# Gate/up in a hybrid encoder layer: five of seven Strassen products with a 512-column operand, six banks per unit, and 63 pieces' sums made in earlier stages

## The chip, the cores and the metric

The kernel runs on one core of one Trainium2 chip. The metric is the device time of one execution, in microseconds (us); lower is better. The time before is the median of three runs.

## The reference, cut to what matters

One layer over 512 tokens of width 2048, in float32: norm, one input projection, two mixers beside each other (dilated window attention with 16 heads of 64, and bidirectional gated linear attention with 4 heads), output projection, norm, and a SwiGLU block of hidden width 5632.

```python
h = rmsnorm(x, attn_norm_w)
aq, ak, av, gq, gk, gv, gr, glr = split(h @ w_in)
attn    = mixture_of_dilations(aq, ak, av, rel_bias_table)      # 16 heads
gla_out = rmsnorm_per_head(gla_fwd + gla_bwd) * gla_norm_w * silu(gr)   # 4 heads
x = x + concat(attn, gla_out) @ w_out
h = rmsnorm(x, ffn_norm_w)
x = x + (silu(h @ w_gate) * (h @ w_up)) @ w_down       # 2048 -> 5632 -> 2048
return rmsnorm(x, final_norm_w)
```

## The kernel before, in words

**Precision.** Every large product is made of three matmuls in a rounded 32-bit format (F32R in the code): an operand is split into a rounded part (hi) and the remainder (lo), and hi x hi, hi x lo and lo x hi are added in the same bank. ACT makes the hi part with a copy, DVE the lo part with a subtraction.

**Stages.** The program is one order of instructions, written out by hand. Jobs 0 to 15 (`run_job`) are the input projection (q/k, v, the operands of linear attention, its output gate) and the output projection. A job has 16 "halves": 128 rows of the weights times 512 columns, made from a 512 KB piece that `Stream` loads on SP's queue, at most three pieces ahead, and splits three halves ahead (L198 on ACT, L199 on DVE). Its products are L295 to L297 or L304 to L306, with 512 columns. Between two halves, `run_side` lets a queue of generators (`side`) make steps of attention or linear attention at a rate per job, and one step from `urgent`.

Job 6 starts at 344.3 us of the span, job 7 at 406.6, job 8 at 464.8, job 12 at 683.3, job 15 at 817.5. The steps in jobs 6 and 7 are the attention of heads 12 to 15, those of jobs 8 to 11 linear attention. Then comes gate/up (862.8 to 1752.6 us of the span), then the down projection and the last norm.

**Attention.** A step (`att_step`, h is the head and b one of its four blocks of queries) has the score matmuls (L573, L574), the score operation on DVE (L586), the transposes of the two steps before (L532) with copies by ACT (L598) and remainders by DVE (L599), the product with V (L540, L541), the exponential by ACT, the mix of an output (L550, L552) and the normalisation (L525, L526). Behind job 5, q and k parts of the last heads are split and copied into place by 24 DMAs on SP's queue (L483 to L495).

**Linear attention.** Per head, the reciprocal root of a mean square is made by a chain of small operations (L323 to L329), which scales an output tile on ACT (L885); TensorE then transposes that (L891).

**Gate/up.** `Feed` goes through 44 units, a 256-column strip of w_gate and one of w_up in turn, and each unit through 4 pieces of 512 x 256 weights. The product is a Strassen-Winograd one: 7 products of quarter blocks in place of 8. Of the weights, each piece needs sums of its blocks (`sums`, L1157 to L1159, three operations on DVE for four sums), and then the split of three blocks and four sums (L1170 on ACT, L1175 on DVE). Of x, `pair_operands` makes the sums and splits during the output projection. A piece has 2 x 7 products of three matmuls with 256 columns (L1216 to L1218):

```python
mm(o, wh, xh, ...)    # L1216
mm(o, wh, xl, ...)    # L1217
mm(o, wl, xh, ...)    # L1218
```

The seven products of a unit lie in four of the eight banks of PSUM, two halves of a bank side by side in three of them. At a unit's end `evac` (L1227, L1232, L1235) empties them in two steps from `urgent`, and a third (`finish`, L1253 to L1259) multiplies with the norm's factor, takes Silu (gate), or multiplies the two and stores the tile (`gd`). `run` sets the order: piece i's split, the sums of pieces i+1 and i+2, the split of i+1, products of i, then one step from `urgent`.

**Buffers.** `s4` has 16 buffers of 1024 columns (in the profile "b"), `s2` 70 of 512 columns ("a"), `ps` the 8 banks. A request takes a free buffer, and the instruction that fills it waits until the last user is done. Each engine and each queue works in its program order.

Of the kernel before, what the change touches and what calls it, by code (L numbers as in the profile page):

```python
# [117 lines left out]
def layer(nc, tc, x, attn_norm_w, w_in, rel_table, gw_f, gb_f, gw_b, gb_b, gla_norm_w, w_out,  # L118
# [7 lines left out]
    with tc.manual_schedule(), \  # L126
# [27 lines left out]
        state = {"credit": 0.0, "set": None}  # L154
# [96 lines left out]
        class Job:  # L251
# [3 lines left out]
            banks = None  # L255

# [11 lines left out]
        def run_job(j):  # L268
# [6 lines left out]
            for i in range(j.n):  # L275
# [754 lines left out]
        def pair_operands(q, fs_):  # L1030

            a, z = slice(0, 256), slice(256, 512)
            f1, f2 = fs_
            t13, t24 = s2.get(), s2.get()
            sub = lambda o, x_, y_: dve.tensor_tensor(o, x_, y_, op=OP.subtract)
            sub(t13.t[:, a], f1.t[:, a], f1.t[:, z])
            sub(t13.t[:, z], f2.t[:, z], f1.t[:, z])
            dve.tensor_tensor(t24.t[:, a], f2.t[:, z], t13.t[:, a], op=OP.add)
            sub(t24.t[:, z], t24.t[:, a], f2.t[:, a])
            yield  # L1040
            todo = []
            slots = []
            for src, n in ((f1.t[:, a], 256), (f2.t, 512), (t13.t, 512), (t24.t, 512)):
                sl, hi, lo, hf = half_split(src, n)
                slots += sl
                todo.append((src, hi, lo, hf))
            for i in range(4):
                src, hi, lo, hf = todo[i]
                act.copy(hi, src)
                sub(lo, src, hf)  # L1050
                put((f1, f2, t13, t24)[i])
                if i % 2:
                    yield
            (_, b1h, b1l, _), (_, f2h, f2l, _), (_, t13h, t13l, _), (_, t24h, t24l, _) = todo
            xs[q] = dict(slots=slots, B11=(b1h, b1l), B21=(f2h[:, a], f2l[:, a]), B22=(f2h[:, z], f2l[:, z]),
                         T1=(t13h[:, a], t13l[:, a]), T3=(t13h[:, z], t13l[:, z]),
                         T2=(t24h[:, a], t24l[:, a]), T4=(t24h[:, z], t24l[:, z]))
# [63 lines left out]
        class Blocks:  # L1121
# [10 lines left out]
            def load(self):  # L1132
                while self.n_load < self.n and len(self.raw) < self.most and s4.free:
                    w, k, n_kt, col, n = self.source(*self.seq[self.n_load])
                    r = s4.get(F32, self.shape(4))
                    sp.dma_start(out=r.t.rearrange("p a b c -> p (a b c)").rearrange("p (k c) -> p k c", k=n_kt),
                                 in_=w[k * P:(k + n_kt) * P, col:col + n].rearrange("(k p) c -> p k c", p=P))
                    self.raw[self.n_load] = r
                    self.n_load += 1

# [40 lines left out]
        class Feed(Blocks):  # L1181
# [3 lines left out]

            def __init__(self):
# [4 lines left out]
                self.begin(seq, 2, P)  # L1191

# [3 lines left out]

            def products(self, i, banks):
                st_ = self.sets.pop(i)
                piece = self.seq[i][1]
                first, last = piece == 0, piece == self.per - 1  # L1200
                a, z = slice(0, 256), slice(256, 512)
                A, B, C, E = (b.t for b in banks)
                for p in range(2):
                    q = 2 * piece + p
                    (rh, rl), (sh, sl) = st_
                    R = lambda n: (rh.t[:, p, n], rl.t[:, p, n])
                    Z = lambda n: (sh.t[:, p, n], sl.t[:, p, n])
                    x_ = xs[q]
                    prods = [(A[:, a], R(0), x_["B11"], True), (A[:, z], R(2), x_["B21"], False),
                             (B[:, a], Z(2), x_["T2"], True), (C[:, a], Z(1), x_["T1"], True),  # L1210
                             (C[:, z], Z(0), x_["T3"], False), (E[:, a], Z(3), x_["B22"], True),
                             (E[:, z], R(1), x_["T4"], False)]
                    for o, (wh, wl), (xh, xl), head in prods:
                        head = head and first and p == 0
                        end = last and p == 1
                        mm(o, wh, xh, start=head, stop=False, skip_group_check=True)  # L1216
                        mm(o, wh, xl, start=False, stop=False, skip_group_check=True)  # L1217
                        mm(o, wl, xh, start=False, stop=end, skip_group_check=True)  # L1218
                for hi, lo in st_:
                    put(hi, lo)  # L1220

            def evac(self, u, banks):
# [12 lines left out]
                dve.tensor_tensor(t1.t[:, z], t1.t[:, a], B[:, a], op=OP.subtract)  # L1235
                yield
# [7 lines left out]
                put(banks[1])  # L1244
                self.finish(u, c_, c)
                yield

            def finish(self, u, c_, c):
                w, j = self.units[u]
                if w is w_gate:  # L1250
                    tables(SILU)
                    for f in range(2):
                        dve.tensor_tensor(c_.t[:, f], c_.t[:, f], rb[2 + f].t, op=OP.mult)  # L1253
                    act.activation(c_.t, c_.t, AF.Silu)
                    self.gate = c_
                else:
                    dve.tensor_tensor(c_.t, c_.t, self.gate.t, op=OP.mult)
                    put(self.gate)
                    pool.dma_start(out=gd[j], in_=c)  # L1259
                    put(c_)  # L1260

            def run(self):
                banks = {}
                for i, (u, q) in enumerate(self.seq):
                    if u not in banks:
                        banks[u] = [ps.get() for _ in range(4)]
# [6 lines left out]
                    if i < 2:  # L1273
                        self.sums(self.n_sums, halves=True)
                    self.products(i, banks[u])
                    if u == len(self.units) - 1:
                        for p in (2 * q, 2 * q + 1):
                            put(*xs.pop(p)["slots"])
                        down_start(q)
                    for _ in range(3 if i < 2 else 2 if i < 8 else 1):  # L1280
                        run_urgent()
                    if q == self.per - 1:
                        urgent.append(self.evac(u, banks.pop(u)))
# [422 lines left out]
        run_last = finish()  # L1706
        for n, j in enumerate(jobs):
# [6 lines left out]
            if n == n_out:  # L1714
                ff.run()
# [29 lines left out]
```

## Time and profile before

| what | value |
|---|---|
| median of 3 runs | 2216.93 us (2216.35 to 2217.04) |
| the profiled execution | 2216.53 us |
| its span | 2214.8 us |
| mean granted TensorE clock | 0.999 |
| TensorE busy | 2204.3 us, 100% of the span |
| VectorE (DVE) busy | 1623.5 us, 73% |
| ScalarE (ACT) busy | 1003.0 us, 45% |
| GpSimd (POOL) busy | 96.0 us, 4% |
| read from / written to HBM | 246.58 MB / 40.70 MB |

How to read it: the time is that of the execution with the profiler, and the span is the stretch from its first instruction to its last; 1.7 us lie around it. PE is TensorE's matmuls, PEld its weight loads, SP the engine that issues most DMAs. L12 is line 12 of the kernel. In the lines of single instructions, the columns are the start and the duration in us, the engine, the line, the operation, output and inputs by the program's names, partitions x elements, the count, and, in brackets, idle time before it with what ended it. In the lines of DMAs they are names, queue, kind and count, KB of each, and the us from issue to landing.

### The profile page before, as it was taken

To read this page: it belongs to the slowest core of one execution; us is meant where nothing else is said; L and a number is where in the kernel's file an instruction comes from. 1 tells how busy PE (TensorE), PEld (TensorE's weight loads), DVE (VectorE), ACT (ScalarE), POOL (GpSimd) and SP (SyncE) were. 2 spreads that over 40 slices of the span, in tenths; PEclk is the share of its full clock that TensorE was granted. 3 is DMA by queue.
4 is the path that set the end of the run, shared out by engine and by line. 5 is a ranking of instruction groups with operands and counts; after the bars stand their busy time and mean duration, and the time that the engine had idled before them with its cause. 6 is when DMAs were issued, how large, how long until landed. Compare 5 with 4: busy or idle time off the path is not lost.

```text
span 2214.8 us, 37040 instructions
## 1 busy us (share of the span) xinstructions
PE 2204.3 (100%) x14842; PEld 2040.1 (92%) x14842; DVE 1623.5 (73%) x2740; ACT 1003.0 (45%) x1664; POOL 96.0 (4%) x149
## 2 busy tenths in 40 slices
PE   9999999999999999999999999999999999999998
PEld 7888888888888888999999999999999999999987
DVE  4366665745454438988888888888888888888795
ACT  5244444444444345444434343444343465565462
POOL 0000000000000100000000000000000010011300
PEclk9999999999999999999999999999999999999999
DMA  6525625231324332334334333343333775575982
GB/s 207 162 82 158 169 87 141 76 124 57 96 67 153 131 127 77 115 115 124 115 115 124 115 124 115 115 125 115 115 125 115 249 164 179 167 195 143 288 316 76
DMA packets 210185, 302.26 MB, mean 136 GB/s; under 512 B 15005, under 2 KB 133197, under 8 KB 210014
## 3 DMA queue, kind: packets, MB, share of 16 engines
q1 hardware_dynamic: 194366, 258.87, 37.3%
q0 software_dynamic: 15328, 40.51, 7.2%
q8 instruction: 116, 1.90, 0.4%
q10 hardware_dynamic: 320, 0.53, 0.1%
q14 instruction: 55, 0.45, 0.1%
HBM read 246.58 MB, written 40.70 MB: 130 GB/s over the span
## 4 chain that ended last, share of the span: by engine, by line
PE 99%; DVE 1%; DMA 0%; SPq 0%; ACT 0%; issue 0%; DVEq 0%
PE ps L1217 13%; PE ps L1216 13%; PE ps L1218 13%; PE ps L304 7%; PE ps L306 7%; PE ps L305 7%; PE ps L297 5%; PE ps L295 5%; PE ps L296 5%; PE ps L1457 5%; PE ps L1456 5%; PE ps L1455 5%; PE ps L532 1%; PE ps L872 1%; PE ps L541 1%; PE ps L540 1%
## 5 line engine op out<-in xcount | busy, mean ns | idle before, releaser
L1216 PE MATMUL ps<-a,b 128*128 128x256 f32 x2464 | 697.5, 283 | 0.0
L1217 PE MATMUL ps<-a,b 128*128 128x256 f32 x2464 | 697.3, 283 | 0.0
L1218 PE MATMUL ps<-a,b 128*128 128x256 f32 x2464 | 697.3, 283 | 0.0
L1170 ACT CAST b<-b 128x1024 fp32r<-128x1024 f32 (+1 forms) x473 | 438.7, 941 | 529.1 <-DVE b L1175 280.6
L1175 DVE TENSOR_TENSOR b<-b,b 128x1024 fp32r<-128x1024 f32 (+1 forms) x473 | 501.5, 1087 | 123.3 <-PE ps L1217 61.6
L1217 PEld LDWEIGHTS ps<-a,b 128*128 128x128 f32 x2464 | 473.1, 192 | 0.0
L1216 PEld LDWEIGHTS ps<-a,b 128*128 128x128 f32 x2464 | 473.1, 192 | 0.0
L1218 PEld LDWEIGHTS ps<-a,b 128*128 128x128 f32 x2464 | 473.1, 192 | 0.0
L199 DVE TENSOR_TENSOR a<-b,a 128x512 fp32r<-128x512 f32 x292 | 194.7, 686 | 132.6 <-ACT a L198 121.5
L1456 PE MATMUL ps<-b,a 128*128 128x256 f32 x896 | 253.6, 283 | 0.0
L1457 PE MATMUL ps<-b,a 128*128 128x256 f32 x896 | 253.6, 283 | 0.0
L1455 PE MATMUL ps<-b,a 128*128 128x256 f32 x896 | 253.6, 283 | 0.0
L198 ACT CAST a<-b 128x512 fp32r<-128x512 f32 x292 | 170.8, 618 | 31.9 <-DMA b<-in_w_in_dram 10.9
L304 PE MATMUL ps<-a,a 128*128 128x512 f32 x464 | 182.7, 394 | 0.0
L305 PE MATMUL ps<-a,a 128*128 128x512 f32 x464 | 180.8, 390 | 0.0
L306 PE MATMUL ps<-a,a 128*128 128x512 f32 x464 | 180.7, 390 | 0.0
L1455 PEld LDWEIGHTS ps<-b,a 128*128 128x128 f32 x896 | 172.0, 192 | 0.0
L1456 PEld LDWEIGHTS ps<-b,a 128*128 128x128 f32 x896 | 172.0, 192 | 0.0
L1457 PEld LDWEIGHTS ps<-b,a 128*128 128x128 f32 x896 | 172.0, 192 | 0.0
L1157 DVE TENSOR_TENSOR b<-b 128x512 f32<-128x512 f32 x233 | 159.5, 684 | 10.8 <-DMA b<-in_w_down_dram 10.8
L295 PE MATMUL ps<-a,a 128*128 128x512 f32 x416 | 167.3, 402 | 0.0
L297 PE MATMUL ps<-a,a 128*128 128x512 f32 x416 | 163.0, 392 | 0.1
(240 smaller groups left out, 3059.7 us busy)
## 6 DMA issues: line engine op xcount, KB each, us to landing
b<-in_w_gate_dram SPq DMA_DIRECT2D x88, 512.0 KB, 3.5
b<-in_w_up_dram SPq DMA_DIRECT2D x88, 512.0 KB, 3.9
b<-in_w_down_dram SPq DMA_DIRECT2D x88, 512.0 KB, 4.9
b<-in_w_in_dram SPq DMA_DIRECT2D x48, 512.0 KB, 4.0
b<-in_w_in_dram SPq DMA_DIRECT2D x92, 256.0 KB, 4.4
b<-in_w_out_dram SPq DMA_DIRECT2D x32, 512.0 KB, 5.5
a<-a SPq DMA_DIRECT2D x96, 128.0 KB, 2.3
gd<-b POOLq DMA_DIRECT2D x22, 512.0 KB, 3.2
```

What stands on the lines that cost most here:

```text
L295: mm(o, wh.t[:, c], xh.t, start=first, stop=False)
L304: mm(o, xh.t[:, c], wh.t[:, w], start=first and not on, stop=False, skip_group_check=on)
L305: mm(o, xh.t[:, c], wl.t[:, w], start=False, stop=False, skip_group_check=on)
L306: mm(o, xl.t[:, c], wh.t[:, w], start=False, stop=last, skip_group_check=on)
L1170: act.copy(o, src)
L1175: dve.tensor_tensor(o, src, h, op=OP.subtract)
L1216: mm(o, wh, xh, start=head, stop=False, skip_group_check=True)
L1217: mm(o, wh, xl, start=False, stop=False, skip_group_check=True)
L1218: mm(o, wl, xh, start=False, stop=end, skip_group_check=True)
L1455: mm(o, xh[:, t], wh, start=first and h == 0, stop=False, skip_group_check=True)
L1456: mm(o, xh[:, t], wl, start=False, stop=False, skip_group_check=True)
L1457: mm(o, xl[:, t], wh, start=False, stop=last, skip_group_check=True)
```

## The change

Three parts belong together.

1. *Gate/up's products.* For units from the third on, five of the seven products get a bank of their own with 512 columns: hi and lo of that part of x lie side by side (`[P, 2, 256]`), and one matmul with 512 columns takes the weights' hi part times both; a second, of 256 columns, adds weights' lo times x's hi to the left half. The last two products (T1 and T3) keep three matmuls of 256 columns and share a sixth bank. A unit so holds six banks; the first two units stay as they were. The order of the seven products is R0, R2, R1, Z2, Z3, Z1, Z0.
2. *Emptying.* `evac5` adds the two halves of each wide bank. Its first part (three ACT copies, seven DVE operations, banks 0 to 4) is put right behind the unit's products, its second (the sixth bank) and the rest one step per piece from `urgent`. `finish` is split into two steps for gate. `pair_operands` makes the x operands in the new layout.
3. *Early sums.* For 63 of the 176 pieces, the weights' sums are made ahead of time: `ahead` loads the piece on SP's queue, makes four additions in place on DVE (each 256 wide) and stores the result to a scratch tensor `sd` on POOL's queue. `run_job` takes 2.4 such additions behind each half's products in jobs 6 to 11, and 1.0 in jobs 12 to 14, ahead of the steps of `run_side`. In gate/up `sums` of such a piece is one DMA, issued three pieces ahead, in place of three DVE operations.

```diff
+                state["ahead"] += j.ahead
+                while state["ahead"] >= 1:
+                    state["ahead"] -= 1
+                    next(state["sums"], None)
                 if i < j.n - 1:
                     state["credit"] += j.rate
                     ...
                     run_side(n)
...  pair_operands
+            for n, (name, f, h) in enumerate((("B11", f1, a), ("B21", f2, a), ("B22", f2, z), ("T2", t24, a),
+                                              ("T4", t24, z))):
+                o = s2.get(F32R, [P, 2, 256])
+                act.copy(o.t[:, 0], f.t[:, h])
+                sub(o.t[:, 1], f.t[:, h], o.f[:, 0])
...  Feed
+                self.pre = {i: n for n, i in enumerate(
+                    i for i, (u, q) in enumerate(seq) if u > 1 and (q == 1 or q == 2 and u % 2))}
+            def ahead(self):
+                todo, held = deque(self.pre), deque()
+                def load():
+                    if todo and len(held) < 2 and len(s4.free) > 1:
+                        r = s4.get(F32, self.shape(4))
+                        self.read(todo[0], r)
+                        held.append((todo.popleft(), r))
+                load()
+                yield
+                while todo or held:
+                    load()
+                    if not held:
+                        yield
+                        continue
+                    i, r = held.popleft()
+                    b = lambda n: r.t[:, :, n]
+                    for o, x_ in ((1, 0), (0, 2), (2, 1), (3, 2)):
+                        dve.tensor_tensor(b(o), b(o), b(x_), op=OP.add)
+                        yield
+                    pool.dma_start(out=self.sd[self.pre[i]], in_=r.t.rearrange("p a b c -> p (a b c)"))
+                    put(r)
+            def sums(self, i, halves=False):
+                if i in self.pre and i == self.n_sums:
+                    self.n_sums += 1
+                    S = s4.get(F32, self.shape(4))
+                    self.S[i] = [S]
+                    sp.dma_start(out=S.t.rearrange("p a b c -> p (a b c)"), in_=self.sd[self.pre[i]])
+                else:
+                    Blocks.sums(self, i, halves)
...  products
+                for n, (kind, b, x) in enumerate(self.PRODUCTS):
+                    for p in range(2):
...
+                        if u > 1 and n < 5:
+                            o = banks[n].t
+                            mm(o, wh, x_.rearrange("p s t -> p (s t)"), ...)
+                            mm(o[:, 0:256], wl, xh, ...)
+                        else:
...
+                            mm(o, wh, xh, ...); mm(o, wh, xl, ...); mm(o, wl, xh, ...)
...  evac5
+                m1, m2, t4, t2, b22, n = (b.t for b in banks)
+                act.copy(t.t[:, a], m1[:, a])
+                act.copy(c[:, 512:768], t4[:, a])
+                act.copy(c[:, 256:512], b22[:, a])
+                add(t.t[:, a], t.t[:, a], m1[:, z])
+                add(c[:, a], m2[:, a], t.t[:, a])
+                add(c[:, a], c[:, a], m2[:, z])
+                add(c[:, 512:768], c[:, 512:768], t4[:, z])
+                sub(t.t[:, z], t.t[:, a], t2[:, a])
+                sub(t.t[:, z], t.t[:, z], t2[:, z])
+                add(c[:, 256:512], c[:, 256:512], b22[:, z])
+                put(*banks[0:5])
+                yield
+                add(v.t..., n..., t.t[:, None, z].to_broadcast([P, 2, 256]))
+                add(c[:, 768:1024], n[:, a], v.t[:, z])
+                put(banks[5])
+                add(c[:, 256:768], c[:, 256:768], v.t)
...  run
-                        banks[u] = [ps.get() for _ in range(4)]
+                        banks[u] = [ps.get() for _ in range(6 if u > 1 else 4)]
+                    if i + 3 in self.pre:
+                        self.sums(i + 3)
                     self.products(i, banks[u])
+                    if q == self.per - 1:
+                        done = (self.evac5 if u > 1 else self.evac)(u, banks.pop(u))
+                        if u:
+                            next(done)
                     for _ in range(...): run_urgent()
+                    if done:
+                        urgent.append(done)
+            j.ahead = 2.4 if 6 <= n < 12 else 1.0 if 12 <= n < n_out else 0.0
```

More of the change, by code (lines that the diff above doesn't have):

```diff
@@ L153, in layer @@
         EXP_LN, SILU = "natural_log_exp_and_others", "silu_and_others"
-        state = {"credit": 0.0, "set": None}
+        state = {"credit": 0.0, "set": None, "ahead": 0.0}
         class Stream:
@@ L255, in layer @@
             banks = None
+            ahead = 0.0
         def job(kind, pieces, kts, acts, evac, rate=0.0, before=None, start=None, limit=None):
@@ L1200, in products @@
                 first, last = piece == 0, piece == self.per - 1
-                a, z = slice(0, 256), slice(256, 512)
[L1202 to L1218, printed above, removed]
@@ L1235, in evac @@
                 dve.tensor_tensor(t1.t[:, z], t1.t[:, a], B[:, a], op=OP.subtract)
+                put(banks[1])
                 yield
@@ L1243, in evac @@
                 yield
-                put(banks[1])
-                self.finish(u, c_, c)
+                yield from self.finish(u, c_, c)
                 yield
@@ L1706, in layer @@
         run_last = finish()
+        state["sums"] = ff.ahead()
+        for n, j in enumerate(jobs):
+            j.ahead = 2.4 if 6 <= n < 12 else 1.0 if 12 <= n < n_out else 0.0
         for n, j in enumerate(jobs):
@@ L1714, in layer @@
             if n == n_out:
+                assert next(state["sums"], None) is None
                 ff.run()
```

89 lines of the change are left out of this document (61 added, 28 removed).

## The prediction

> **What bounds the kernel now.** I read the page's busy times and chain first, then the stages (busy time by window), then the order of time inside the stages that the change touches.
>
> ```profile
> PE 2204.3 (100%) x14842; PEld 2040.1 (92%) x14842; DVE 1623.5 (73%) x2740; ACT 1003.0 (45%) x1664; POOL 96.0 (4%) x149
> PE 99%; DVE 1%; DMA 0%; SPq 0%; ACT 0%; issue 0%; DVEq 0%
> L1216 PE MATMUL ps<-a,b 128*128 128x256 f32 x2464 | 697.5, 283 | 0.0
> ```
> ```profile
> 1000.00:1200.00 200.00, 200.00 (x1669) 200.00 (x1668) 174.68 (x265) 80.95 (x94) 2.67 (x5) 1.00 0.38 118
> 344.30:374.00 29.70, 29.70 (x135) 22.85 (x134) 13.44 (x26) 9.56 (x19) 0.00 (x0) 1.00 0.66 171
> 374.00:450.00 76.00, 76.00 (x402) 64.52 (x401) 52.83 (x119) 39.00 (x84) 0.00 (x0) 1.00 0.31 97
> 500.00:683.00 183.00, 183.00 (x865) 154.03 (x864) 91.53 (x166) 82.02 (x181) 7.37 (x14) 1.00 0.27 85
> ```
>
> The chain is TensorE for 99% of the span. In the windows (length, then PE, PEld, DVE, ACT, POOL, granted clock, DMA share, GB/s) TensorE never rests at a full clock. So time goes only if TensorE issues less, and every wait that the change puts in front of TensorE is paid in full, wherever it lies. The first window is gate/up (DVE 87% busy), the next two are the job with the last q/k halves and the attention of heads 12 to 15 (DVE 45%, then 70%), the fourth is the gated linear attention (DVE 50%). The sums that the change moves go from the first of these into the other three.
>
> **Gain: fewer matmuls.** What one costs is the distance of starts, not the 283 ns of the row.
>
> ```profile
> 700.26 0.39 PE L304 MATMUL ps<-a,a 128*128 128x512 f32 x1
> ...
> 700.94 0.39 PE L304 MATMUL ps<-a,a 128*128 128x512 f32 x1
> ...
> 382.02 0.39 PE L574 MATMUL ps<-a,a 128*128 128x512 f32 x1
> 382.25 0.28 PE L540 MATMUL ps<-b,b 128*128 128x256 f32 x1
> ...
> 383.08 0.28 PE L541 MATMUL ps<-b,b 128*128 128x256 f32 x1
> 383.20 0.40 PE L295 MATMUL ps<-a,a 128*128 128x512 f32 x1
> ```
>
> 256 columns take 120 ns (1669 in the 200 us of the gate/up window), 512 take 227 (0.68 us for three), and the last two pairs show that mixing them changes neither: 0.23 from a 512 to a 256, 0.12 from a 256 to a 512. Two of 256 therefore cost 240, one of 512 costs 226.7: 13.3 ns less. The change merges five pairs for each of 2 halves of 4 pieces in 42 units, 1680 merges: 1680 x 13.3 = **22.4 us** gained (21.8 with the rounded 227). A piece goes from 5.04 to 42 x 0.120 - 10 x 0.0133 = 4.91 us, a unit from 20.16 to 19.63.
>
> The Trainium skill ("TensorE: Matmul & The Clock Gate", Back-to-back issue gap) gives a warm matmul N/2.4 + 2.5 ns, which makes a merge worth 2.5 ns and all of them 4.2 us. The trace disagrees: 120 and 227 lie 13.3 above N/2.4, so I keep 22.4.
>
> **Gate/up: does it stay covered?**
>
> ```profile
> 1290.04 0.42 DVE L1227 TENSOR_TENSOR b<-ps,a 128x256 f32<-128x256 f32 x1
> 1290.37 0.41 DVE L1235 TENSOR_TENSOR a<-a,ps 128x256 f32<-128x256 f32 x1
> 1290.70 0.69 DVE L1157 TENSOR_TENSOR b<-b 128x512 f32<-128x512 f32 x1
> 1291.42 0.43 DVE L1158 TENSOR_TENSOR b<-b,b 128x256 f32<-128x256 f32 x1
> 1291.89 0.43 DVE L1159 TENSOR_TENSOR b<-b,b 128x256 f32<-128x256 f32 x1
> ...
> 1293.94 2.10 DVE L1175 TENSOR_TENSOR b<-b,b 128x768 fp32r<-128x768 f32 x2 [1.63 <-PE ps L1217]
> ```
>
> By distance of starts a 256-wide op takes 0.33 us, 0.47 where it waits for the one before, a 512-wide one 0.72, so a piece's sums 1.5; a split's two ops take 2.1. The new emptying has seven 256-wide ops in its first part (3 x 0.47 + 4 x 0.33 = 2.7) and 0.72 + 0.33 + 0.72 = 1.8 in its second: 4.5 per unit, where the old one has 2.4 (3 x 0.33 + 2 x 0.72). Three of eight sums leave each gate/up pair of units. From the window's 87.3%, DVE works 35.2 of a pair's 40.3 us; it will work 35.2 - 3 x 1.5 + 2 x 2.1 = 34.9 of 39.3. The first part is queued behind the split of the last piece, which starts with that piece, 4.9 us before the unit's end: it runs from -2.9 to about -0.2. Its banks are finished at -4.2, -3.5, -2.8, -2.1 and -1.4, as the products come bank by bank. The next unit starts in two spare banks and needs the first emptied one at +1.39. That is 1.6 us or more of cover, so I cost it at nothing; without it each 0.1 us costs 42 x 0.1 = 4.2. The worst piece after it (a gate unit's first: sums, split, second part, 5.4 us in 4.9) has its split ready 1.4 us early. The read-back of finished sums is asked for two pieces (9.8 us) before use; the nearest row, of the same size and kind, is the b<-gd one below, 7.6 us.
>
> **Cost: the early sums.** 63 pieces, each a 512 KB load on SP's queue, four 256-wide adds on DVE and a store on POOL's. The jobs 6 to 11 take 2.4 adds behind each half's products, about 0.40 us each, ahead of that half's step of attention or linear attention. Nothing is prefetched: the loader asks for at most one piece per call, so that the first call (one buffer free) fails and every later piece is asked for directly before its first add. Where many buffers are free (5 to 9 from the end of attention on) SP runs ahead and the load is early anyway. In the attention of jobs 6 and 7 only 1 to 4 are free. DVE takes its work in order, so an add without its data stops everything behind it.
>
> ```profile
> b<-in_w_gate_dram SPq DMA_DIRECT2D x88, 512.0 KB, 3.5
> ...
> b<-gd SPq DMA_DIRECT2D x22, 512.0 KB, 7.6
> ...
> b<-in_w_in_dram SPq DMA_DIRECT2D x1, 512.0 KB, 6.9
> ```
> ```profile
> 350.90 0.47 SPq L483 DMA_DIRECT2D a<-a  x1
> ...
> 367.48 0.59 SPq L495 DMA_DIRECT2D a<-a  x1
> ...
> 378.36 0.69 DVE L586 CUSTOM_DVE_ANT_0 a<-ps,b 128x512 f32<-128x512 f32 x1 [0.36 <-PE ps L574]
> 378.96 0.48 PE L295 MATMUL ps<-a,a 128*128 128x512 f32 x1
> ...
> 379.42 1.29 DVE L599 TENSOR_TENSOR b<-ps,b 128x512 fp32r<-128x512 f32 x2 [0.36 <-ACT b L598]
> ...
> 382.45 0.69 DVE L586 CUSTOM_DVE_ANT_0 a<-ps,b 128x512 f32<-128x512 f32 x1 [0.55 <-PE ps L574]
> ...
> 386.40 0.49 DVE L526 TENSOR_SCALAR a<-a,small 128x512 f32<-128x512 f32 x1
> 386.41 1.19 PE L532 MATMUL ps<-idn,a 128*128 128x128 f32 x8
> ```
>
> A landing takes 3.5 us, or 6.9 for the one 512 KB load that was issued between 344 and 374, where DMA is 66% busy; these are its two ends. Issue and release add about 0.5.
>
> *Lead-in.* Between 350.9 and 368.1 SP issues 24 copies of q and k parts and little else. Three early loads stand among them and the fourth behind them, and some copies in turn need remainders that DVE makes behind an early add. Step by step: load 2 goes out at 354.6, lands at 358 to 361.5, and the copies behind it are 2 to 5 us late; load 3 goes out at 366.4 to 369, lands at 370 to 374; load 4 at 375.4 to 379.4, lands at 379 to 384. DVE then still has 3.6 us (with a copy by ACT between) to the remainder of the weights that the job's ninth half multiplies by (that half starts at 378.96, and its third matmul reads it 0.45 later), so TensorE waits 3.5 to 7 us, the first new stall. The score op of step (12,0), at 378.4 before, comes at 388 to 392, the V product behind it with it: TensorE is now 8 to 12 late. Load 6 takes a buffer freed by the remainder just in front of its add, so DVE stands for the whole landing: 14 to 18 late at the transposes that ran at 386.41. There the trace of before has no reserve at all: the L526 that they need ended at 386.89.
>
> *The other steps.* A step took 4.1 us (378.36 to 382.45), a pair 8.2, with 0.91 idle ahead of its two L586 (0.36 and 0.55); 4.8 adds x 0.40 = 1.9 don't fit, and with the wait for ACT that vanishes (0.36) 0.6 remains: 8 pairs, 5 us. Load 10 has its add ahead of job 6's four evictions: DVE stands 3 to 4 us, and the next score matmul waits for one of those banks. The other loads land in time once DVE is late. Together 9.
>
> Attention therefore costs 23 to 27 us; I take **25**, nearer the short landing, which most rows have. The bound below is what an exact fit would leave, nothing; above, 6.9 for every load, 31.
>
> *Linear attention.*
>
> ```profile
> 508.70 0.61 ACT L198 CAST a<-b 128x512 fp32r<-128x512 f32 x1
> ...
> 509.34 0.69 DVE L199 TENSOR_TENSOR a<-b,a 128x512 fp32r<-128x512 f32 x1 [8.61 <-ACT a L198]
> ...
> 509.95 0.17 DVE L323 TENSOR_SCALAR small<-small 128x4 f32<-128x4 f32 x1
> ...
> 511.42 1.57 ACT L885 ACTIVATE b<-ps,small 128x256 f32<-128x256 f32 x4 [0.83 <-DVE small L329]
> ...
> 513.05 1.03 PE L891 MATMUL ps<-idn,b 128*128 128x128 f32 x8
> ```
>
> The chain L323 to L885 ends at 512.99, 0.06 before TensorE uses it. In the changed order two (or three) adds stand between that L199 and L323: 0.8 to 1.2 us later, 0.7 to 1.1 of it on TensorE, for each of 4 heads: **3.2 us**.
>
> POOL works 4% of the span; its 63 stores stand in front of nothing that the traces show late: nothing. The operand splits of x (one 512-wide pair fewer, four 256-wide more per pair of tiles) lie in the output projection, whose DVE is half idle: nothing, 1 us at most.
>
> **Sum.** The profiled execution took 2216.5 us (span 2214.8 and 1.7 around it), 0.4 under the median of 2216.9. 2216.5 - 22.4 + 25 + 3.2 = 2222.3: **2222 us**, slower by 0.25%. About 0.2% (4.4 us) is what a measurement of this kernel can tell from no change.
>
> **Rivals.**
> *The early sums are hidden* (faster). For it: DVE is idle 16 us between 344 and 374 and 23 between 374 and 450, and 45 adds are only 18. Against it: the adds stand in front of a chain without reserve. If half of the waits go, 2216.5 - 22.4 + 14 = 2208; if all go, 2194. It decides from a loss under 18 us: 30%.
> *A draw*: the landings stay at 3.5 and adds overlap more; loss 18 to 26.8, 2212.1 to 2220.9: 19%.
> *TensorE waits for banks at the unit's border*, on top of my sum: decides if the first part ends over 1.6 us later than worked out, say because the split waits for buffers. At 0.3 us a border 42 x 0.3 = 12.6: 2235. For it: DVE 89% busy. Against: rows of before show the split at the piece's start. 7%.
> *The skill's formula above* for mixed widths (gain 4.2): 2240; the 0.23 and 0.12 us rows speak against it: 2%.
> My forecast, slower with the loss in attention: 42%, by itself 2221 to 2230.
>
> So faster 0.30, same 0.19, slower 0.51. The range leaves out about one in ten on either side: 2202 (most of the waits hidden) to 2235 (long landings, or small border waits).
>
> **What would show it.** Right: starts in gate/up 227 and 120 ns apart and the stage near 867 us instead of 890; DVE adds with idle time put down to DMA from in_w_gate and in_w_up between 344 and 460; transposes of the attention released by the line of the normalisation in front of them; the attention of heads 12 to 15 ending some 25 us later. Wrong: no idle time of TensorE before 470 us, or gaps at each first use of an emptied bank.

## The result, and the profile after

The changed kernel takes 2254.4 us against 2216.5 us before: 1.0173 times as long, interval 1.016 to 1.0186. The prediction had 2222, range 2202 to 2235: the sign was right, the size was not (its sum came to 5.8 us more, 37.9 were measured).

First the page of the changed kernel: busy times, and the chain that ended last.

```profile
PE 2208.0 (98%) x13162; PEld 1956.9 (87%) x13162; DVE 1703.4 (76%) x3029; ACT 1030.8 (46%) x1764; POOL 129.1 (6%) x212
PE 86%; DVE 5%; issue 4%; DMA 3%; SPq 1%; ACT 1%; POOL 0%; DVEq 0%; POOLq 0%; ACTq 0%
L1264 PE MATMUL ps<-a,b 128*128 128x512 f32 x1680 | 601.7, 399 | 0.3
L1266 PE MATMUL ps<-a,b 128*128 128x256 f32 x1680 | 472.3, 281 | 0.5 <-DVE b L1185 0.5
```

1680 matmuls fewer, and yet more busy time of TensorE (2208.0 against 2204.3). The chain now lies off TensorE for 14% of a longer span, most of it on DVE, DMA and "issue" (time in which an engine waited for nothing that the profile shows). Then the windows of the stages (length, PE, PEld, DVE, ACT, POOL busy, granted clock, DMA share, GB/s): job 6, job 7, jobs 8 to 11, gate/up.

```profile
343.40:431.80 88.40, 69.22 (x306) 54.79 (x305) 47.33 (x108) 27.39 (x57) 4.27 (x8) 0.86 0.61 183
431.80:499.90 68.10, 60.90 (x300) 50.31 (x299) 49.63 (x118) 27.13 (x57) 5.32 (x10) 0.97 0.67 223
499.90:730.40 230.50, 223.40 (x1034) 185.49 (x1033) 167.24 (x354) 97.89 (x214) 24.85 (x48) 0.99 0.75 254
909.90:1790.10 880.20, 879.38 (x5736) 799.79 (x5735) 762.65 (x1208) 396.52 (x537) 12.63 (x24) 1.00 0.48 158
```

By the first product of each stage, that is 26.1 us more for job 6 (62.3 before), 10.0 more for job 7 (58.1), 12.0 more for jobs 8 to 11 (218.4), and 9.3 less for gate/up (889.5). The three terms of the prediction's sum were 25 for jobs 6 and 7 together, 3.2 and 22.4. All three were too favourable.

The stages of all kernels that follow, in us, are taken from each one's profile in the same way, with the time of the whole (the median; e4, e5, e9, e11 and e13 were run once):

| kernel | job 6 | job 7 | jobs 8-11 | jobs 12-15 | gate/up | whole |
|---|---|---|---|---|---|---|
| before | 62.3 | 58.1 | 218.4 | 179.4 | 889.5 | 2216.5 |
| changed | 88.4 | 68.1 | 230.4 | 179.4 | 880.2 | 2254.4 |
| e1 grouped | 86.4 | 70.1 | 231.1 | 179.4 | 872.6 | 2248.7 |
| e2 no early sums | 62.3 | 58.1 | 218.4 | 179.4 | 917.9 | 2243.9 |
| e3 late | 62.3 | 58.1 | 220.7 | 209.1 | 880.7 | 2237.6 |
| e4 transfers only | 62.5 | 58.1 | 218.4 | 179.4 | 879.7 | 2206.4 |
| e5 additions, stores unpaced | 87.1 | 61.7 | 226.0 | 179.4 | 879.7 | 2241.5 |
| e9 the same, other buffers | 90.1 | 61.8 | 227.8 | 179.4 | 878.4 | 2245.2 |
| e11 additions alone, paced | 67.7 | 61.8 | 227.8 | 205.0 | 878.4 | 2248.2 |
| e6 loader ahead | 73.5 | 66.9 | 230.1 | 179.4 | 880.2 | 2238.9 |
| e10 behind the steps | 71.7 | 69.1 | 222.5 | 179.4 | 880.8 | 2233.4 |
| e13 loads on POOL's queue | 104.4 | 104.1 | 413.2 | 196.2 | 878.4 | 2503.9 |
| e7 42 pieces | 62.3 | 58.1 | 221.2 | 185.8 | 897.0 | 2231.1 |
| e8 spread | 62.4 | 58.1 | 222.4 | 179.6 | 874.4 | 2213.7 |
| e12 spread, behind the steps | 62.3 | 58.1 | 220.0 | 179.4 | 873.8 | 2202.2 |

**Gate/up.** The order of time on TensorE in the changed kernel, over the ten merged pairs of one piece:

```profile
1002.66 0.40 PE L1264 MATMUL ps<-a,b 128*128 128x512 f32 x1
1002.90 0.28 PE L1266 MATMUL ps<-a,b 128*128 128x256 f32 x1
1003.01 0.40 PE L1264 MATMUL ps<-a,b 128*128 128x512 f32 x1
...
1006.08 0.28 PE L1266 MATMUL ps<-a,b 128*128 128x256 f32 x1
1006.19 0.28 PE L1272 MATMUL ps<-a,b 128*128 128x256 f32 x1
```

Ten pairs take 1006.19 - 1002.66 = 3.53 us, 353 ns each. Three matmuls of 256 columns took 360, and the prediction had 347 for the pair. So a merge gains 6.7 ns instead of 13.3: 1680 x 6.7 = 11.2 us, of which 9.3 arrived. TensorE rests 0.8 us in this stage (880.2 less 879.4); the other 1.1 are not placed.

**Attention.** The order of time on DVE and on SP's queue (L1235 is an early addition, L1148 an early load; lines are 5 to 6 further than before), and what DVE waited for between 343 and 500 us (in all, how often, the longest):

```profile
362.85 0.69 DVE L199 TENSOR_TENSOR a<-b,a 128x512 fp32r<-128x512 f32 x1
375.37 0.88 DVE L1235 TENSOR_TENSOR b<-b 128x256 f32<-128x256 f32 x2 [11.84 <-DMA b<-in_w_up_dram]
376.17 0.68 DVE L483 TENSOR_TENSOR a<-a,a 128x512 fp32r<-128x512 f32 x1
```
```profile
367.72 0.59 SPq L491 DMA_DIRECT2D a<-a  x1
368.36 0.59 SPq L1148 DMA_DIRECT2D b<-in_w_up_dram  x1
```
```profile
DVE b L1235 <- DMA b<-in_w_up_dram: 28.7, 8, 11.8
DVE b L1235 <- DMA b<-in_w_gate_dram: 12.7, 3, 9.4
```

An addition that DVE reached at 363.5 stands until 375.4, because its load only goes out at 368.36, behind the copies of q and k (L491 and those before it), and then takes 7.0 us to the addition. The next piece repeats it: its load goes out at 382.01, behind copies (L499, L500) that needed the remainder made at 376.17, and its addition stands until 387.70.

```profile
382.01 0.62 SPq L1148 DMA_DIRECT2D b<-in_w_gate_dram  x1
387.70 0.42 DVE L1235 TENSOR_TENSOR b<-b 128x256 f32<-128x256 f32 x1 [9.45 <-DMA b<-in_w_gate_dram]
```

On TensorE, the first of these waits and its end, and the end of the second, look like this:

```profile
371.57 0.39 PE L297 MATMUL ps<-a,a 128*128 128x512 f32 x1
377.51 0.79 PE L298 MATMUL ps<-a,a 128*128 128x512 f32 x1 [5.55 <-DVE a L199]
378.10 0.63 PE L296 MATMUL ps<-a,a 128*128 128x512 f32 x1
378.53 0.63 PE L297 MATMUL ps<-a,a 128*128 128x512 f32 x1
...
391.53 0.80 PE L296 MATMUL ps<-a,a 128*128 128x512 f32 x1 [9.39 <-ACT a L198]
```

The windows behind the two stops (columns as above):

```profile
377.50:381.60 4.10, 4.09 (x10) 3.13 (x10) 0.72 (x2) 0.00 (x0) 0.53 (x1) 0.50 0.81 237
391.50:396.90 5.40, 5.37 (x13) 4.21 (x14) 5.19 (x10) 3.49 (x6) 0.53 (x1) 0.50 0.14 56
```

5.7 us of rest, and then 512 columns take 0.43 us instead of 0.227: the granted clock is 0.50 for the next 4 us, and again for 5 us after the next stop, of 9.8 us. Added up over all starts of jobs 6 and 7, the waits over 0.38 us make 28.1 us, and the smaller excesses, nearly all of them at the lower clock, 8.3 us: 36.4, where the stages give 36.1.

### The profile page after: what moved, and what is told of

It is laid out like the page before. It is cut to its first block, busy times and chain, and to the rows that moved or that the text cites. A ratio compares the mean times of both kernels' runs of the same rounds, so it can differ in the third digit from the quotient of the medians.

```text
span 2252.7 us, 34805 instructions
## 1 busy us (share of the span) xinstructions
PE 2208.0 (98%) x13162; PEld 1956.9 (87%) x13162; DVE 1703.4 (76%) x3029; ACT 1030.8 (46%) x1764; POOL 129.1 (6%) x212
## 4 chain that ended last, share of the span: by engine, by line
PE 86%; DVE 5%; issue 4%; DMA 3%; SPq 1%; ACT 1%; POOL 0%; DVEq 0%; POOLq 0%; ACTq 0%
PE ps L1264 17%; PE ps L1266 9%; PE ps L307 6%; PE ps L305 6%; PE ps L306 6%; PE ps L1553 5%; PE ps L1552 5%; PE ps L1551 5%; PE ps L1273 4%; PE ps L1274 4%; PE ps L1272 4%; PE ps L296 3%; PE ps L298 3%; PE ps L297 3%; DMA b<-in_w_up_dram 2%
## 5 line engine op out<-in xcount | busy, mean ns | idle before, releaser
L1180 ACT CAST b<-b 128x1024 fp32r<-128x1024 f32 (+1 forms) x473 | 433.1, 942 | 483.1 <-DVE b L1185 329.6
L1264 PE MATMUL ps<-a,b 128*128 128x512 f32 x1680 | 601.7, 399 | 0.3
L1266 PE MATMUL ps<-a,b 128*128 128x256 f32 x1680 | 472.3, 281 | 0.5 <-DVE b L1185 0.5
L1264 PEld LDWEIGHTS ps<-a,b 128*128 128x128 f32 x1680 | 316.2, 188 | 71.6 <-PE ps L1266 0.8
L1266 PEld LDWEIGHTS ps<-a,b 128*128 128x128 f32 x1680 | 317.7, 189 | 0.8 <-DVE b L1185 0.8
L1273 PE MATMUL ps<-a,b 128*128 128x256 f32 x784 | 222.1, 283 | 0.0
L1274 PE MATMUL ps<-a,b 128*128 128x256 f32 x784 | 222.0, 283 | 0.0
L1272 PE MATMUL ps<-a,b 128*128 128x256 f32 x784 | 221.6, 283 | 0.0
L296 PE MATMUL ps<-a,a 128*128 128x512 f32 x416 | 169.7, 408 | 10.2 <-ACT a L198 10.2
```

The lines of the kernel that those rows point to most:

```text
L1180: act.copy(o, src)
L1264: mm(o, wh, x_.rearrange("p s t -> p (s t)"), start=first and p == 0, stop=False, skip_group_check=True)
L1266: mm(o[:, 0:256], wl, xh, start=False, stop=end, skip_group_check=True)
```

## The experiments

### Which part costs what

**e1: the same matmuls in another order.** Inside a piece, the wide matmuls of a group of products first, then the narrow ones.

```diff
-for each product n of 0..4, each half p:  wide(n, p); rest(n, p)
+for group in ((0, 1, 2), (3, 4)) if not last piece else ((0,), (1,), (2,), (3,), (4,)):
+    for part in (wide, rest):
+        for n in group:
+            for p in range(2): part(n, p)
```

> The changed kernel with another order of the same matmuls inside a piece of gate/up: all 512-wide ones of a group of products first, then its 256-wide ones (two groups in a unit's first three pieces, one product at a time with both halves in its last piece). Theory (each change from 512 to 256 columns and back costs 6.7 ns together): 11 such changes per unit instead of 40, so 29 x 42 x 6.7 ns = 8.2 us less, gate/up 872 us instead of 880, the whole 2246. Rival (the price belongs to the wide matmul or to writing one bank twice, whatever its neighbours): gate/up stays at 880, the whole 2254. Second rival (the banks are finished later and the emptying is then late): more than 2254.

Gate/up 872.6 us, 7.6 less than the changed kernel, as the theory had it. The order of time, the six wide and the six narrow ones of a group, then the four of the next:

```profile
1002.46 1.55 PE L1264 MATMUL ps<-a,b 128*128 128x512 f32 x6
1003.85 0.88 PE L1267 MATMUL ps<-a,b 128*128 128x256 f32 x6
1004.56 1.09 PE L1264 MATMUL ps<-a,b 128*128 128x512 f32 x4
```

1.39 us for six of 512 and 0.71 for six of 256 are 2.10 for six pairs, 350 ns each, against 353 in alternation; with 11 changes per unit instead of 40 the gain over before is 16.9 us instead of 9.3. The order of the matmuls thus carries part of the price. It does not carry all of it: six wide ones in a row still take 1.39 / 6 = 0.232 us each, where the jobs take 0.227, and about half of the 6.7 ns per pair stays (350 against 347) although the width now changes only between groups. And in the attention of the kernel before, the 32 steps from 512 to 256 columns and the 32 back take 227 and 120 ns on average, the same as without a change. There a change of width has no price, so the reason that the theory gave is not shown.

**e2: no early sums.**

```diff
-self.pre = {... if u > 1 and (q == 1 or q == 2 and u % 2)}
+self.pre = {}
```

> The changed kernel without its early sums: wide products and six banks stay, every piece's sums are made inside gate/up as before. Theory: jobs 6 to 11 take again what they took before (48 us less), gate/up has 35.2 + 4.2 = 39.4 us of DVE work in 39.9 us of TensorE work per gate/up pair and just fits: 2206 us, gate/up 880. Rival: DVE is then the bound of gate/up, stalls at units' borders of 1 us and more: 42 x 1 = 42 us, gate/up 920, the whole 2248.

The rival. Jobs 6 to 11 are as before to 0.1 us, so the early sums are the whole loss there. But gate/up takes 917.9 us. The window of the stage, and the chain:

```profile
862.30:1780.00 917.70, 900.22 (x5735) 798.49 (x5734) 844.08 (x1396) 391.70 (x537) 12.62 (x24) 1.00 0.37 115
PE 62%; DVE 32%; issue 4%; ACT 1%; DMA 0%; DVEq 0%; SPq 0%
```

DVE, 92% busy, holds up TensorE; my sum of 39.4 us in 39.9 was no fit. The wide products need the early sums: 917.9 against 880.2.

**e4: the early transfers without the additions.**

```diff
-dve.tensor_tensor(b(o), b(o), b(x_), op=OP.add)
```

> The changed kernel without the 252 early additions: the loads, the stores and the read-back stay as they are (gate/up computes with unsummed blocks). Theory (DVE standing behind the landings is the loss): jobs 6 to 11 take nearly what they took before, 2206 to 2210 us. Rival (the loads on SP's queue delay the q/k copies and the prefetch of the weights by themselves): jobs 6 and 7 still lose 10 us or more, 2217 to 2235.

As the theory had it: jobs 6 to 11 lose 0.2 us in all, and the whole is 2206.4. The 63 loads and 63 stores cost next to nothing as long as DVE doesn't wait for them. The third and fourth early load go out at 364.10 and 372.24 here, where they went out at 368.36 and 382.01.

**e3: the sums later.**

```diff
-j.ahead = 2.4 if 6 <= n < 12 else 1.0 if 12 <= n < n_out else 0.0
+j.ahead = 1.6 if 8 <= n < 12 else 3.25 if 12 <= n < n_out else 0.0
```

> The changed kernel with the same 63 pieces' sums made later: none in jobs 6 and 7, 1.6 additions per half in jobs 8 to 11, 3.25 in jobs 12 to 14. Theory (DVE stands in its own order behind loads that find no free buffer in the attention of heads 12 to 15): jobs 6 and 7 take 120 us as before (36 us less), jobs 8 to 11 lose 8 to 12 us, jobs 12 to 14 nothing or a few: 2217 us. Rival (each early addition costs its 0.4 us wherever it stands, 48 us for 252 less what overlaps): 2240 to 2254. Second rival (the rates in jobs 12 to 14 fill DVE there): jobs 12 to 14 longer by over 10.

Jobs 6 and 7 as before, jobs 8 to 11 lose only 2.3, but jobs 13 and 14 take 58.0 and 61.1 us instead of 45.3: the second rival, though not by DVE's own work. Jobs 12 and 13 of that kernel, by window, and what DVE waits for between 727 and 850:

```profile
683.00:727.00 44.00, 44.00 (x196) 36.44 (x195) 35.97 (x77) 16.57 (x30) 7.38 (x14) 1.00 0.94 333
727.00:785.00 58.00, 48.20 (x209) 38.40 (x209) 38.48 (x90) 18.00 (x40) 11.23 (x21) 0.94 0.97 337
```
```profile
DVE b L1235 <- DMA b<-in_w_up_dram: 36.2, 9, 10.3
```

DMA is 94% to 97% busy at some 335 GB/s; the loads land late and DVE stands before them.

### How the loss in attention divides

**e5 and e9: additions without early loads.** The additions work on one buffer that was loaded once, the stores write another; e9 takes the buffers from the larger pool.

```diff
-    i, r = held.popleft()                 # a piece just loaded
+    i = todo.popleft()                    # r, r2: loaded once
 ...
-    pool.dma_start(out=self.sd[self.pre[i]], in_=r...)
+    pool.dma_start(out=self.sd[self.pre[i]], in_=r2...)
```

> The changed kernel with its 252 early additions at their places and its 63 stores, but without the 63 early loads: the additions work on one buffer that was loaded once, the stores write another (gate/up so gets wrong sums). Theory (standing behind landings, and the clock's fall after each long stand, is most of the loss): jobs 6 and 7 lose 5 to 10 us by DVE's own work, jobs 8 to 11 under 8: 2211 to 2224. Rival (252 additions of 0.4 us are by themselves too much for a DVE that others wait for): jobs 6 to 11 lose over 35 us, 2241 or more.

> The run without early loads once more, with the additions and the stores on four buffers of the other, larger pool, so that none of the 16 is held (gate/up gets wrong sums): the 19 us stand in job 6 of that run came behind copies on SP's queue, which may have been the two held buffers' doing. Theory (landings of the early loads are most of the loss in attention): jobs 6 and 7 lose 5 to 10 us, jobs 8 to 11 7 to 8 as in that run: 2218 to 2225. Rival (the additions by themselves make the q/k remainders and copies late): jobs 6 and 7 lose 20 or more, 2233 and up.

By number both fall to their rival: jobs 6 and 7 lose 28.4 and 31.5 us. But they don't decide it for job 6, by a fault of their making: the stores no longer waited for the additions, and went out as fast as POOL could ask. From e9, the window of job 6's middle and two copies on SP's queue:

```profile
352.00:372.00 20.00, 17.60 (x75) 11.78 (x74) 4.79 (x11) 2.29 (x5) 10.84 (x20) 1.00 1.01 330
```
```profile
352.36 2.11 SPq L490 DMA_DIRECT2D a<-a  x1
354.52 2.16 SPq L491 DMA_DIRECT2D a<-a  x1
```

DMA is full, and SP takes 2.1 us to issue a copy that took it 0.5 to 0.6 before. What they do show is jobs 8 to 11, 7.6 and 9.4 longer.

**e11: additions alone, paced.** As e9, with the stores only behind all additions, from job 13 on.

> Additions alone, paced as in the changed kernel: 252 of them at their places, in two buffers of the larger pool, with no early load and with the stores only in jobs 12 to 15 (gate/up gets wrong sums). In the two runs before of this kind the stores waited for nothing and filled DMA from job 6 on, so that they could not tell. Theory (the landings and SP's queue are most of the loss in attention): jobs 6 and 7 lose 5 to 10 us, jobs 8 to 11 7 to 8: about 2206 + 15 = 2221 if the end is undisturbed, read by the stages. Rival (DVE's own work): jobs 6 and 7 lose 20 or more. Second rival (DVE has room for it): under 3.

Job 6 loses 5.4, job 7 3.7, together 9.1: the theory. Jobs 8 to 11 lose 9.4, a little over the 7 to 8 expected; job 15 pays for the late stores (25.6 us), so the whole says nothing. Of the 36.1 us in attention, then, 9 come with the additions alone, and transfers alone cost 0.2 (e4). The other 27 arise only where additions wait for transfers: waiting for loads, and the clock after it.

**e6: a loader that works ahead.**

```diff
+    if not held or step - held[0][2] < 4:      # asked for less than 4 steps ago
+        step += 1
+        yield
+        continue
     for o, x_ in ((1, 0), (0, 2), (2, 1), (3, 2)):
+        load()
         dve.tensor_tensor(b(o), b(o), b(x_), op=OP.add)
```

> The changed kernel with a loader that works ahead: up to two pieces in hand, and the first addition of a piece stands at least four steps (1.7 halves, 6.5 us) behind the place of its load; rates as they are, 63 pieces. Theory (the load stands directly before its first addition, so that the landing is paid on DVE): the waits on transfers nearly vanish and it comes near the run without loads plus gate/up's 9.4 us of gain, 2212 to 2225. Rival (a buffer taken early is a buffer for which SP's queue and attention wait): jobs 6 and 7 still lose over 25 us, 2240 or more.

In between: jobs 6 and 7 lose 20.0 instead of 36.1. Neither range holds it. DVE's waits for early loads fall from 41.4 to 9.8 us, but others are there. What DVE waited for between 343 and 500 us, two that are new:

```profile
DVE b L604 <- DMA sd<-b: 12.6, 4, 4.8
DVE a L199 <- DMA a<-a: 10.3, 1, 10.3
```

And what TensorE waited for:

```profile
PE ps L546 <- DVE b L604: 8.7, 4, 3.7
```

L604, which fills a buffer for the product with V, stands until a store to the scratch tensor has read that buffer. TensorE's product with V (L546) waits 8.7 us behind it, of the 20.0 lost. So the rival's price for buffers is real, at a little under half of what is left.

**e10: the additions behind the half's step instead of ahead of it.**

```diff
-    state["ahead"] += j.ahead ...; next(state["sums"], None)
     run_side(n)
+    state["ahead"] += j.ahead ...; next(state["sums"], None)
```

> The changed kernel with the early additions of a half behind that half's step of attention or linear attention instead of in front of it. Theory (DVE works in order, so that an addition without data stops the next step instead of this one; in linear attention the short chains of small operations come first): jobs 6 and 7 lose as much within 6 us, jobs 8 to 11 lose 5 to 8 instead of 12: 2248 to 2254. Rival (the place in front of the step is what makes the loss): jobs 6 and 7 recover 15 us or more, 2235 or less.

My theory failed here: job 6 recovers 16.7 us, so the place in front of the step makes most of job 6's loss, as the rival had it, though job 7 recovers nothing. The third early load goes out at 360.01, where it went out at 368.36. The step's remainder for the copies (L479, L483) now stands ahead of the addition on DVE:

```profile
358.21 0.68 DVE L483 TENSOR_TENSOR a<-a,a 128x512 fp32r<-128x512 f32 x1
365.12 0.88 DVE L1235 TENSOR_TENSOR b<-b 128x256 f32<-128x256 f32 x2 [6.23 <-DMA b<-in_w_up_dram]
```
```profile
360.01 1.00 SPq L1148 DMA_DIRECT2D b<-in_w_up_dram  x1
```

In the changed kernel the addition waited for a load, the load stood on SP's queue behind copies, and the copies waited for a remainder that stood behind the addition before: each early load of the lead-in paid for the whole round. Jobs 8 to 11 lose 4.1 instead of 12.0, less than the 5 to 8 expected.

**e13: the early loads on POOL's queue.**

```diff
-self.read(todo[0], r)              # sp.dma_start
+self.read(todo[0], r, pool)        # pool.dma_start
```

> The changed kernel with the early loads on POOL's queue instead of SP's. Theory (in job 6 the early loads stand behind copies and weights on SP's queue, whose inputs DVE makes behind the very additions that wait for the loads): job 6 loses 8 us less or better, 18 or under instead of 26, job 7 about as much: 2240 to 2247. Rival (they wait for buffers, or for DMA, whichever queue asks): job 6 as before within 3 us, 2251 to 2257.

Far outside both: 2503.9 us. POOL's queue:

```profile
364.96 0.55 POOL L1237 DMA_DIRECT2D sd<-b  x1 [9.87 <-DVE b L1235]
365.49 0.76 POOL L1148 DMA_DIRECT2D b<-in_w_up_dram  x1
379.12 0.54 POOL L1237 DMA_DIRECT2D sd<-b  x1 [12.87 <-DVE b L1235]
379.65 0.76 POOL L1148 DMA_DIRECT2D b<-in_w_gate_dram  x1
```

A load stands behind the store of the piece before, and that behind its additions, so no load is ever early, and every job from 6 to 11 takes 102 to 105 us. It doesn't tell whether SP's queue was the fault. It does show what SP gives in jobs 8 to 11: there it runs ahead of DVE (between 500 and 735 us the additions of the changed kernel wait 2.3 us for loads in all), and the loss is 12 us and not 195.

### Does the change pay without its two costs?

**e7: grouped, 42 pieces, none in attention.**

```diff
-... u > 1 and (q == 1 or q == 2 and u % 2)
+... u > 1 and q == 1
+j.ahead = 1.5 if 8 <= n < 12 else 3.25 if n == 12 else 1.0 if 12 < n < n_out else 0.0
```

> Grouped wide matmuls as in the first of these runs; 42 pieces instead of 63 with early sums (the second piece of each unit), none of them in jobs 6 and 7: 1.5 additions per half in jobs 8 to 11, 3.25 in job 12, 1.0 in jobs 13 and 14. Theory: gate/up 872 to 874 us (DVE 34.9 + 1.5 = 36.4 us of work in 39.7 per gate/up pair), jobs 8 to 11 lose 2, the others nothing: 2216.5 - 17 + 2 = 2202. Rival (DVE needs all 63 early to keep gate/up's borders fed): stalls of 0.5 us per unit, 21 us, 2222.

The rival: gate/up 897.0. TensorE's waits between 860 and 1770 us:

```profile
PE ps L1264 <- DVE a L1292: 11.6, 17, 1.4
```

L1292 is in the emptying of the banks: this is the wait at the unit's border that the prediction had as a rival, and it comes as soon as DVE has one more piece's sums per gate/up pair. Job 13 also lost 5.8. The same kernel with the loader of e6 (e7b, expected below) took 2232.3 us, the same within the uncertainty, as its rival had it; it moved the loss from job 13 to job 12 (4.0).

> The same with the loader that works ahead. Theory: what jobs 8 to 14 still lose to landings goes, 0.5 to 2 us less than the one before, about 2200.5. Rival: no landing is waited for there, no difference within 0.1%.

**e8 and e12: grouped, 63 pieces, spread.** Both keep the grouped order, ask for a load two steps ahead, and make no early addition in jobs 2 to 6.

```diff
 e8:  ahead of the half's step
+j.ahead = {0: 0.75, 1: 1.4, 7: 2.0, 12: 2.0, 13: 1.6, 14: 1.6, 15: 1.8}.get(n, 1.6 if 8 <= n < 12 else 0.0)
 e12: behind the half's step
+j.ahead = {7: 2.0, 8: 2.3, 9: 2.3, 10: 2.3, 11: 1.6, 12: 2.4, 13: 1.6, 14: 1.6, 15: 1.5}.get(n, 0.0)
 both: in job 7 only from the twelfth half on
```

> Grouped wide matmuls; all 63 pieces with early sums, spread over the places where buffers are free: 0.75 additions per half in job 0, 1.4 in job 1, 2.0 in job 7 behind its attention, 1.6 in jobs 8 to 11, 2.0 in job 12, 1.6 in 13 and 14, 1.8 in 15, none in jobs 2 to 6; the loader asks two steps ahead. Theory (the loss is one of place: few free buffers and a DVE chain without reserve in jobs 6 and 7, full DMA in the late version's jobs 13 and 14): gate/up 872.6, jobs 8 to 11 lose 3, the others 1 to 2: 2216.5 - 17 + 4.5 = 2204. Rival (DMA is full or landings are waited for in jobs 0, 1 or 12 to 15 too): 5 to 20 us lost there, 2209 to 2224.

2213.7 us, 0.999 of before (0.998 to 0.9999): the rival. Gate/up is 874.4, but jobs 0 and 1 take 2.0 and 4.1 us longer and jobs 8 to 11 4.0.

> Grouped wide matmuls; 63 pieces, none in jobs 0 to 6: 2.0 additions per half in job 7 behind its attention, 2.3 in jobs 8 to 10, 1.6 in 11, 2.4 in 12, 1.6 in 13 and 14, 1.5 in 15, all behind the half's step; the loader asks two steps ahead. Theory: gate/up 873 to 875, jobs 8 to 11 lose 2, nothing else: 2216 - 15.5 + 2 = 2202.5. Rival (DMA or the small chains of linear attention take back as much as in the spread version before): 2210 to 2216.

2202.2 us, 0.9939 of before (0.9922 to 0.9955), as the theory had it. This version beats both kernels. Its gate/up by window, and what TensorE waits for between 343 and 1740 us:

```profile
863.40:1737.00 873.60, 872.08 (x5735) 797.26 (x5734) 761.63 (x1210) 397.00 (x539) 13.35 (x25) 1.00 0.49 159
```
```profile
PE ps L1268 <- DVE a L1296: 1.3, 1, 1.3
PE ps L811 <- DVE a L793: 0.7, 1, 0.7
```

TensorE hardly rests, and the stages around are those of before but for 1.6 us.

## Why the prediction was right or wrong

**Right: what bounds it, the sign, and the mechanism in attention.** TensorE without reserve pays every wait in full, and additions without their data, in DVE's order, were most of the wait. Up to load 3 the lead-in went as the prediction walked it: out at 368.36 (said: 366.4 to 369), the first new stop 5.7 us (said: 3.5 to 7). e4 shows that without the additions almost nothing is lost there, e2 that without the early sums nothing is.

**Wrong: the gain per merge.** The distances were read rightly: in the kernel before, 32 steps from 512 to 256 columns and 32 back average 227 and 120 ns. The step that failed is carrying "mixing them changes neither" from attention to gate/up, where no such sequence had run. The row there showed 353 ns per pair in place of 347, and e1 that grouping gets about half of that back. The term was 22.4 us, and 9.3 arrived. The formula of the Trainium skill ("TensorE: Matmul & The Clock Gate", Back-to-back issue gap) gave 4.2 for this term as an estimate, nearer in number. But the 16.9 us that e1 gains lie far above 4.2, so the rows bear out the larger fixed price per matmul.

**Wrong: the size in attention.** Of 25 us forecast, 28.1 came as waits, above the 23 to 27 of the prediction and under the 31 of its bound. The walk failed at load 4: it went out at 382.01 (said: 375.4 to 379.4), so the second stop was 9.8 us, and the score operation of step (12,0) came at 397.72 (said: 388 to 392). The early loads 2, 3 and 4 took 5.6, 7.0 and 5.7 us to their additions, nearer the 6.9 of the upper bound than the 3.5 that I leaned to. What was not in the sum at all is the clock: 8.3 us of matmuls at half clock after TensorE had stopped. The windows with 0.50 show it. The Trainium skill states it ("TensorE: Matmul & The Clock Gate", Part 1: The HAM clock gate): after an idle window of some 3.4 us the array runs at half clock until it has been busy about as long. The trace agrees, with 0.43 us per matmul for 4 us after a 5.7 us stop. In one place it differs: behind a stop of only 2.6 us, which ended at 694.00, the granted clock was 0.52 for 3.5 us, and there the measurement decides. I had costed only the stops.

**Wrong: linear attention.** 3.2 us forecast at the transposes behind L323 to L329; 12.0 measured. At that place the four heads lost about 0.5 us each, 2. Most of the rest came at a place that I had not walked through: TensorE's masked score products, which wait for DVE's L792. From the changed kernel, what TensorE waits for between 500 and 735 us:

```profile
PE ps L810 <- DVE a L792: 6.0, 3, 2.6
PE ps L296 <- ACT a L198: 0.8, 1, 0.8
```

That L792 ends a chain of a scan, small operations and ACT steps in which each early addition stands in line. Behind the longest of these waits, at the lower clock, matmuls took some 2 us more. The remaining 1 to 2 us are mostly waits for split weights (L296). The chain that I did price was the one that I had found without reserve; there were two. e11 shows 9.4 with the additions alone, and e10 shows that 7.9 go when the step comes first.

**Right: the cover in gate/up, but with less room than the sums said.** With 63 early sums the borders hold (TensorE 879.4 busy of 880.2). With 42 they don't (897.0), without any it is 917.9. My sum that DVE's 34.9 us fit into 39.3 held; the same sum with 39.4 in 39.9 did not, nor did 36.4 in 39.7.

**The rivals.** "The early sums are hidden" was too dear at 30%: it holds for other places (e12), not for jobs 6 and 7. My sum with the measured sizes is 2216.5 - 9.3 + 36.1 + 12.0 = 2255.3; 0.7 of the difference to 2254.4 is a shorter job 0 in that profile.

**What stays open.** Why a pair of 512 and 256 columns takes 353 ns in gate/up and 347 in attention is not shown; the order within a piece is about half of it (e1). It is not the early sums' transfers: in e2, which has none, the median distances are the same (235 and 117 ns, against 236 and 118). How the 27 us beyond e11's 9 divide between buffers and SP's order isn't settled to the us: e6 (loads asked for earlier, 16 recovered) and e10 (order, 15.7 recovered) each get at a part, and they were not run together in attention.

## What to carry to other kernels

An addition placed into another stage is cheap only where its data is there: ask, for each engine and queue in its order, what the load stands behind and whether that in turn waits for the work that waits for the load. Where the bounding engine is stopped for several us, price the slower clock behind the stop too. And before multiplying a distance by thousands, take it from a run of the very sequence that the change makes, in its own stage: 64 good distances from another stage gave 347 where the stage itself gave 353.

## What the runs showed of the hardware that was not expected

- Pairs of 512 and 256 columns: 347 ns in the attention of the kernel before, in gate/up 353 in alternation and 350 with six of each in a row (232 and 118 ns).
- In e9, with DMA full (1.01 of its time, 330 GB/s), SP took 1.6 to 2.2 us to issue most copies, against 0.5 to 0.6. Full DMA alone is not shown to be the reason: in e3, at 0.97 and 337 GB/s, most loads on SP's queue took 0.4 to 0.6 us to issue.
- After a stop of 5.7 us the granted clock was 0.50 for 4 us, after one of 2.6 us 0.52 for 3.5 us; in jobs 6 and 7 the lower clock added 8.3 us to 28.1 us of waits.
